# Where SBUF tiles begin: multiples of 256 bytes, and sixteen operand tiles in steps of 16

## The chip, the cores and the metric

The kernel runs on one NeuronCore of a Trainium2 chip. The metric is the device time in microseconds (us) of one execution. A time is the median of several runs.

## What is computed

A trunk of two decoder layers on 512 tokens of width 1024, batch 1, all in float32:

```python
for i in range(2):
    if i == 0:
        u = rms_norm(h, conv_norm_g)
        h = h + conformer_conv(u, ...)       # pw1 (1024 -> 2048), GLU, causal depthwise conv (31 taps),
    else:                                    # layer norm, SiLU, pw2 (1024 -> 1024)
        u = rms_norm(h, attn_norm_g)
        h = h + diff_attention(u, ...)       # 8 heads, QK norm, T5 bias, two softmaxes per head, w_o
    u = rms_norm(h, ffn_norm_g[i])
    h = h + (silu(u @ w_gate[i]) * (u @ w_up[i])) @ w_down[i]      # 1024 -> 2816 -> 1024
    gate = sigmoid(rms_norm(h, ple_norm_g[i]) @ ple_w_gate[i])
    h = h + gate * (p[i] @ ple_w_proj[i])
```

## The kernel before

**Layout.** Activations are kept transposed: `h[c]`, c = 0..7, holds 128 of the 1024 channels on the partitions and the 512 tokens along the row. A tile of 128x512 float32 takes 2048 bytes of a partition.

**Products in three.** Each float32 operand is split into a high part rounded to float32r and a low part, the remainder. `mm3` (lines 139 to 143) makes one product of them with three matmuls into the same PSUM tile: low x high (line 141), high x low (142), high x high (143). In TensorE's operation one operand is *stationary* (loaded as weights by LDWEIGHTS, 128 columns of it at a time, 512 bytes of a partition) and the other *moves* (512 columns, 2048 bytes of a partition). In nearly all of the kernel the weight matrix is stationary (tiles `whi`, `wlo`, 128x1024, of which column block k is used at step k of the sum) and the activation moves. In the projection to q, k and v (`tokens`) it is the other way round: the norm's tile is stationary, a half of `whi` or `wlo` moves.

**Norm tiles.** A norm (class `Norm`) writes for each chunk c the scaled activation in two tiles, high `A{2c}` and low `A{2c+1}`: sixteen tiles A0 to A15. `split_scaled` (lines 154 to 156) fills them from ScalarE and VectorE. The same sixteen tiles hold the convolution's output ahead of pw2 (`z`) and the heads' outputs ahead of w_o (`ot`, `stage_o`). The hidden activations of an FFN lie in B0 to B7, each with its high and its low half in one buffer of 4096 bytes.

**The stream.** Weights come by DMA on the Sync queue into `wraw` (two buffers), ScalarE rounds them to `whi`, VectorE or GpSimd subtracts to `wlo` (four buffers each). The framework's scheduler orders each engine's instructions; the stages are pw1 with the depthwise convolution between, pw2, the FFN (gate and up, then down, in three parts of 8, 8 and 6 blocks), the gated embedding, then QKV with attention's stages between, w_o, and FFN and embedding again. The last output tile of the kernel is done in two cuts of 256 columns.

**Where tiles begin.** A pool gives each tag its buffers in the order in which the tags first come up, each rounded up to 32 bytes. Ahead of all lie a scratch area of 2048 bytes for DMA descriptors and four constants of 32 each. Then come `vec` (416), `ident` (512), `ones` (512), four `wk` (2048 each) and `mhalf` (32). That makes 11840 = 46 x 256 + 64. The tiles that follow are all of 2048 or 4096 bytes: `h`, `acc`, `wraw`, `whi`, `wlo`, A0 to A15, `wth`, `wtl`, `bias`. So each of these begins 64 bytes past a multiple of 256. Then come the small `v8` and `r8`, two of 32 bytes each, so that `rb`, `big`, C0 to C3, B0 to B7 and D0 to D5 begin 192 bytes past one. C4, which came up earlier, begins at 64; C5, behind the 32 bytes of `lam`, at 224.

Of the kernel before, what the change touches and what calls it, by code (L numbers as in the profile page):

```python
# [13 lines left out]
F32R = mybir.dt.float32r  # L14
# [6 lines left out]
P = 128  # L21
S = 512
# [23 lines left out]
NV = _at  # L46
# [26 lines left out]
def trunk(ctx, tc, xT, pT, wts, diag, dww, vec, rel, onehot, lamv, out):  # L73
    nc = tc.nc
    V, A, G, T = nc.vector, nc.scalar, nc.gpsimd, nc.tensor
# [7 lines left out]
    def sb(shape, tag, bufs, dt=F32):  # L83
        uid[0] += 1
        return pool.tile(shape, dt, tag=tag, name=f"{tag}_{uid[0]}", bufs=bufs)
# [9 lines left out]
    big = lambda dt=F32, shape=(P, S): sb(list(shape), "big", 5, dt)  # L95
    f = lambda ap: ap.bitcast(F32)


    vt = sb([P, NV], "vec", 1)
    nc.scalar.dma_start(vt, vec)  # L100

    def col(name, i=0):
        a, _ = VEC[name]
        return vt[:, a + i : a + i + 1]
# [2 lines left out]
    make_identity(nc, ident)  # L107
    ones_r = sb([P, P], "ones", 1, F32R)
    ones = f(ones_r)
    t = wk()[:, 0:P]  # L110
    V.memset(t, 1.0)
    V.tensor_copy(ones_r, t)
    mhalf = sb([P, 8], "mhalf", 1)
    V.memset(mhalf, -0.5)


    t = tp()
# [36 lines left out]
    def split_scaled(src, scale, hi, lo):  # L154
        A.activation(hi, src, AF.Copy, scale=scale)
        V.scalar_tensor_tensor(lo, src, scale, f(hi), ALU.mult, ALU.subtract)  # L156

    class Norm:
# [4 lines left out]
            self.eng = acc_engine or G  # L163

        def chunk(self, c):
            hi = sb([P, S], f"A{2 * c}", 1, F32R)
            lo = sb([P, S], f"A{2 * c + 1}", 1, F32R)
            split_scaled(h[c], col(self.g, c), hi, lo)
            self.u.append((hi, lo))
            if c == 0:  # L170
                A.activation(self.acc, h[c], AF.Square)
            else:
                sq = wk()
                A.activation(sq, h[c], AF.Square)
                self.eng.tensor_tensor(self.acc, self.acc, sq, ALU.add)  # L175

        def columns(self):

            t = tp()
            for b in range(4):  # L180
                T.matmul(t[:, b : b + 1], self.acc[:, b * P : (b + 1) * P], ones[:, 0:1], start=True, stop=True)  # L181
            return rsqrt_cols(t[:, 0:4], 4, 1.0 / D)
# [11 lines left out]
    last_pow = [None]  # L194

    def rsqrt_cols(src, n, inv):
        v = sb([P, 8], "v8", 2)
        last_v[0] = V.tensor_scalar(v[:, :n], src, inv, EPS, ALU.mult, ALU.add)
        r = sb([P, 8], "r8", 2)
        last_pow[0] = G.tensor_tensor(r[:, :n], v[:, :n], mhalf[:, :n], ALU.pow)  # L200
        return r[:, :n]

# [173 lines left out]
        moments(NC - 2)  # L376
    moments(NC - 1)

    vs = sb([P, 8], "v8", 2)
    junk = wk()  # L380
    for at, t in ((4, sums["mean"]), (0, sums["sq"])):
        for b in range(4):
# [4 lines left out]
    V.tensor_tensor(vs[:, 4:8], vs[:, 4:8], vs[:, 4:8], ALU.mult)  # L387
    V.tensor_tensor(vs[:, 0:4], vs[:, 0:4], vs[:, 4:8], ALU.subtract)
    lrow = spread(diagonal(rsqrt_cols(vs[:, 0:4], 4, 1.0)))
    with tc.issue_after(last_v[0].ins), tc.issue_after(last_pow[0].ins):  # L390
        drow = wk()
# [22 lines left out]
    z = []  # L414
    with tc.manual_schedule(engines={V.engine, A.engine}):
        for c in range(NC + 2):
            if c < NC:
                V.tensor_tensor(y[c], y[c], lrow, ALU.mult)
                A.activation(y[c], y[c], AF.Silu, scale=col("ln_g", c), bias=col("ln_b", c))
                z.append((sb([P, S], f"A{2 * c}", 1, F32R), sb([P, S], f"A{2 * c + 1}", 1, F32R)))  # L420
                A.copy(z[c][0], y[c])
            if c >= 2:
                V.tensor_tensor(z[c - 2][1], y[c - 2], f(z[c - 2][0]), ALU.subtract)
# [139 lines left out]
    def tokens(ws, tb, between=()):  # L563
        acc = mm()
        for k in range(NC):
            a = tuple(t[:, tb * P : (tb + 1) * P] for t in u[k])
            mm3(acc, a, ws[k], k == 0, k == NC - 1)
            if k < len(between) and between[k]:
                between[k]()
        if rcol[0] is None:  # L570
            r = sb([P, 4], "rcol", 1)
            V.tensor_copy(r, norm.columns())
            rcol[0] = r
        return acc, rcol[0][:, tb : tb + 1]
# [15 lines left out]
    def unit(pair, ws, tb, between):  # L590

        if tb == 0:
            qk[pair] = [sb([P, 2, S], f"C{i}", 2, F32R) for i in range(6)]

            for c in range(2):
                G.memset(f(qk[pair][4 + c][HALVES[1 - c]]), 0.0)  # L596
        acc, r = tokens(ws, tb, between)
        q = big()
        A.activation(q, acc, AF.Copy, scale=r)
        sq = wk()  # L600
        if SQ_ACT:
            A.activation(sq, acc, AF.Square, scale=r)
        else:
            G.tensor_tensor(sq, q, q, ALU.mult)
        ss = sb([P, 8], "v8", 2)
        V.tensor_reduce(out=ss, in_=sq.rearrange("p (g d) -> p g d", g=8), op=ALU.add, axis=AX.X)
        rs = rsqrt_cols(ss, 8, 1.0 / DH)
        q3 = q.rearrange("p (g d) -> p g d", g=8)
        G.tensor_tensor(q3, q3, rs.unsqueeze(2).to_broadcast([P, 8, DH]), ALU.mult)
        return pair, tb, q  # L610
# [78 lines left out]
    def stage_a(hd, qb):  # L689
        if qb % 2 == 0:  # L690
            oacc[hd, qb // 2] = mm()
        o = oacc[hd, qb // 2][:, (qb % 2) * 2 * P : (qb % 2 + 1) * 2 * P]
        hi, lo = state[hd, qb]
        for k in range(qb + 1):
            cut = slice(k * P, (k + 1) * P)
            T.matmul(o, hi[:, cut], val[hd, k], start=(k == 0), stop=False)  # L696
            T.matmul(o[:, 0:P], lo[:, cut], val[hd, k][:, 0:P], start=False, stop=(k == qb))  # L697
        if qb % 2 == 1:
            if qb == 1:
                osb[hd] = sb([P, S], f"D{hd % 6}", 1)  # L700
            half = osb[hd][:, (qb // 2) * 2 * P : (qb // 2 + 1) * 2 * P].rearrange("p (a d) -> p a d", a=2)
            t4 = oacc[hd, qb // 2].rearrange("p (a c d) -> p a c d", a=2, c=2)
            A.copy(half, t4[:, :, 1])
            V.tensor_tensor(half, t4[:, :, 0], half, ALU.add)
        if qb == 3:
            o_ = osb[hd]
            sq = wk()
            A.activation(sq, o_, AF.Square)
            ss = sb([P, 8], "v8", 2)
            V.tensor_reduce(out=ss[:, 0:4], in_=sq.rearrange("p (g d) -> p g d", g=4), op=ALU.add, axis=AX.X)  # L710
            r0 = sb([P, 4], "r0", 1)
            V.reciprocal(r0, stats[hd][:, :, 2])
            V.tensor_tensor(ss[:, 0:4], ss[:, 0:4], r0, ALU.mult)
            V.tensor_tensor(ss[:, 0:4], ss[:, 0:4], r0, ALU.mult)
            rs = rsqrt_cols(ss[:, 0:4], 4, 1.0 / P)
            V.tensor_tensor(rs, rs, r0, ALU.mult)
            o3 = o_.rearrange("p (g d) -> p g d", g=4)
            G.tensor_tensor(o3, o3, rs.unsqueeze(2).to_broadcast([P, 4, P]), ALU.mult)
# [3 lines left out]
    def stage_o(hd):  # L722
        t = tp()
        for i in range(4):
            T.transpose(t[:, i * P : (i + 1) * P], osb[hd][:, i * P : (i + 1) * P], ident)  # L725
        hi = sb([P, S], f"A{2 * hd}", 1, F32R)
        lo = sb([P, S], f"A{2 * hd + 1}", 1, F32R)
        split_scaled(t, gains[:, 1:2], hi, lo)
        ot[hd] = (hi, lo)

# [3 lines left out]
    for n in range(len(todo) + LA):  # L734
        for stage, at in ((stage_s, n), (stage_t, n - LT), (stage_a, n - LA)):
            if 0 <= at < len(todo):
                stages.append((n, partial(stage, *todo[at])))
# [6 lines left out]
    for what, at, pace in QKV:  # L744
        ws = slab(GLO if at > 0 else 0)
        for tb in range(4):
            between = take(3 * pace[tb])
            between += [None] * (6 - len(between))
            if waiting:
                between.append(partial(unit_end, *waiting))  # L750
                waiting = None
            if what == "v":
                values(at, ws, tb, between)
            else:
                waiting = unit(at, ws, tb, between)
# [5 lines left out]
    def step():  # L761
        if stages:
            n, s = stages.pop(0)
            s()
        else:
            n = 99
        while done[0] < NH and (n - LA - 3) // 4 > done[0]:
            stage_o(done[0])
            done[0] += 1
# [150 lines left out]
```

## Time and profile before

| | |
|---|---|
| median of 3 runs | 1330.34 us (1330.23 to 1330.62) |
| profiled execution | 1331.2 us |
| its span, first to last instruction | 1329.4 us |
| mean granted TensorE clock | 0.983 |
| TensorE (PE) busy | 1291.5 us, 97% |
| weight loads (PEld), beside PE | 1038.7 us, 78% |
| VectorE (DVE) busy | 778.4 us, 59% |
| ScalarE (ACT) busy | 547.7 us, 41% |
| GpSimd (POOL) busy | 303.3 us, 23% |

In the profile's rows a matmul's tiles are written `mm<-A,whi`: the PSUM tile, then the tiles read, with their buffer numbers left out. L141 is line 141 of the kernel. `xN` is a count. In rows of groups, "| 425.4, 395" is the busy time of the group in us and the mean length of one in ns. In rows of the timeline the first number is the start in us, the second the length. Matmuls overlap: one starts before the previous has ended, so their pace is read from the distance of starts.

### The profile page before, as it was taken

Reading aid. Unit: us, or ns where it says so; the run is one execution under the profiler, and the core shown is the slowest. Engines: PE = TensorE matmul, PEld = TensorE weight load, DVE = VectorE, ACT = ScalarE, POOL = GpSimd, SP = SyncE. Lnnn points to the kernel's source line nnn. Section 1 sums busy time; section 2 is a strip of 40 time slices with the busy share of each in tenths; the row PEclk is TensorE's granted clock in tenths of the full one; section 3 lists DMA queues with packets and bytes.
Section 4 is the critical chain, followed back from the end, with each engine's and each line's share of the span. In section 5 each row is a group of like instructions: output and inputs, shape, how many; then the busy total and the mean of one; then the engine's idle time right before and its main releaser. Section 6 shows DMA issues by size and latency. Waiting matters only on the chain. (4 is left out here: it accounts for less than half of the span.)

```text
span 1329.4 us, 15025 instructions
## 1 busy us (share of the span) xinstructions
PE 1291.5 (97%) x5686; PEld 1038.7 (78%) x5686; DVE 778.4 (59%) x1203; ACT 547.7 (41%) x862; POOL 303.3 (23%) x241
## 2 busy tenths in 40 slices
PE   8999879999999999999999998999999999999998
PEld 6766458888888888888888886878888888888887
DVE  6999984644344434455678897946543344334445
ACT  5676453422123222244466766734322222223332
POOL 5789842100000000022254544122000000000030
PEclk7999889999999999999999999899999999999999
DMA  6231113233333332233222221213333233222231
GB/s 221 91 102 51 51 32 96 89 100 97 95 96 96 95 95 95 80 103 102 86 64 85 98 80 47 89 40 119 96 97 97 94 103 101 96 94 89 78 120 64
DMA packets 37332, 120.40 MB, mean 91 GB/s; under 512 B 4323, under 2 KB 5475, under 8 KB 37260
## 3 DMA queue, kind: packets, MB, share of 16 engines
q1 hardware_dynamic: 35712, 117.06, 27.5%
q10 hardware_dynamic: 1548, 2.39, 0.6%
q8 instruction: 44, 0.72, 0.2%
q14 instruction: 28, 0.23, 0.1%
HBM read 117.31 MB, written 2.12 MB: 90 GB/s over the span
## 5 line engine op out<-in xcount | busy, mean ns | idle before, releaser
L135 ACT CAST whi<-wraw 128x1024 fp32r<-128x1024 f32 (+2 forms) x214 | 218.4, 1025 | 568.2 <-PE mm L143 367.1
L141 PE MATMUL mm<-A,wlo 128*128 128x512 f32 (+1 forms) x1096 | 427.3, 394 | 10.4 <-POOL C L596 5.8
L142 PE MATMUL mm<-A,whi 128*128 128x512 f32 (+1 forms) x1096 | 430.0, 393 | 0.3 <-DVE A L156 0.3
L143 PE MATMUL mm<-A,whi 128*128 128x512 f32 (+1 forms) x1096 | 428.2, 391 | 0.0
L136 DVE TENSOR_TENSOR wlo<-wraw,whi 128x1024 fp32r<-128x1024 f32 (+2 forms) x207 | 258.9, 1254 | 63.2 <-ACT whi L135 63.0
L141 PEld LDWEIGHTS mm<-A,wlo 128*128 128x128 f32 x1096 | 207.8, 190 | 57.1 <-POOL C L596 6.6
L175 POOL TENSOR_TENSOR acc<-acc,wk 128x512 f32<-128x512 f32 x42 | 68.4, 1628 | 790.5 <-issue 676.8
L142 PEld LDWEIGHTS mm<-A,whi 128*128 128x128 f32 x1096 | 208.1, 190 | 46.3 <-issue 2.8
L143 PEld LDWEIGHTS mm<-A,whi 128*128 128x128 f32 x1096 | 207.8, 190 | 44.6 <-issue 1.9
L143 PE MATMUL mm<-B,whi 128*128 128x512 f32 x352 | 139.1, 395 | 0.0
L142 PE MATMUL mm<-B,whi 128*128 128x512 f32 x352 | 139.0, 395 | 0.0
L141 PE MATMUL mm<-B,wlo 128*128 128x512 f32 x352 | 138.4, 395 | 0.0
L304 POOL TENSOR_TENSOR wk<-wk,C 128x512 f32<-128x512 f32 x76 | 111.4, 1470 | 26.7 <-ACT C L303 20.6
L479 DVE TENSOR_TENSOR h<-mm,h 128x512 f32<-128x512 f32 x48 | 33.0, 692 | 128.0 <-PE mm L143 127.8
L471 DVE TENSOR_TENSOR big<-mm,rb 128x512 f32<-128x512 f32 x44 | 30.4, 691 | 125.9 <-PE mm L143 125.9
L469 DVE TENSOR_TENSOR big<-mm,rb 128x512 f32<-128x512 f32 x44 | 30.4, 691 | 99.4 <-PE mm L143 93.0
L143 PEld LDWEIGHTS mm<-B,whi 128*128 128x128 f32 x352 | 66.1, 188 | 16.1
L142 PEld LDWEIGHTS mm<-B,whi 128*128 128x128 f32 x352 | 66.1, 188 | 16.0
L141 PEld LDWEIGHTS mm<-B,wlo 128*128 128x128 f32 x352 | 66.1, 188 | 16.0
L143 PE MATMUL mm<-whi,A 128*128 128x512 f32 x192 | 75.6, 394 | 0.0
L142 PE MATMUL mm<-wlo,A 128*128 128x512 f32 x192 | 75.0, 396 | 0.0
L141 PE MATMUL mm<-whi,A 128*128 128x512 f32 x192 | 74.8, 396 | 0.0
(185 smaller groups left out, 1439.0 us busy)
## 6 DMA issues: line engine op xcount, KB each, us to landing
wraw<-in_wts SPq DMA_DIRECT2D x194, 512.0 KB, 3.5
wraw<-in_wts SPq DMA_DIRECT2D x16, 384.0 KB, 3.1
h<-in_xT SPq DMA_DIRECT2D x8, 256.0 KB, 5.8
bias<-scr ACTq DMA_DIRECT2D x8, 256.0 KB, 3.4
D<-in_diag SPq DMA_DIRECT2D x7, 256.0 KB, 4.0
out_t<-h SPq DMA_DIRECT2D x7, 256.0 KB, 2.0
wraw<-in_wts SPq DMA_DIRECT2D x4, 256.0 KB, 5.1
wraw<-in_pT SPq DMA_DIRECT2D x4, 256.0 KB, 2.6
```

What stands on the lines that cost most here:

```text
L135: A.copy(hi[:, cut], raw[:, cut])
L136: eng.tensor_tensor(lo[:, cut], raw[:, cut], f(hi[:, cut]), ALU.subtract)
L141: T.matmul(acc, al, bh, start=first, stop=False)
L142: T.matmul(acc, ah, bl, start=False, stop=False)
L143: return T.matmul(acc, ah, bh, start=False, stop=last)
L175: self.eng.tensor_tensor(self.acc, self.acc, sq, ALU.add)
L304: G.tensor_tensor(pacc, pacc, pr, ALU.add)
L469: V.tensor_tensor(tg, pg, rb, ALU.mult)
L471: V.tensor_tensor(tu, pu, rb, ALU.mult)
L479: V.tensor_tensor(h[m], acc, h[m], ALU.add)
```

## The change

Scratch and small tiles are padded so that every large tile begins at a multiple of 256 bytes: the scratch shrinks to 1024 bytes, `vec` gets 896, `mhalf` 1024 and is allocated (and set) ahead of `wk`, `v8` and `r8` get 256 for each buffer. Together, 1024 + 128 + 896 + 512 + 512 + 1024 = 4096, where `wk` begins. (The two buffers of tag C5, allocated behind `lam`, begin 32 bytes past a multiple.) The sixteen A tiles get 2304 bytes each, nine times 256, and tile i uses the 2048 that begin 16 x i bytes into them. So A0 begins at a multiple of 256, A1 16 bytes past one, and A15 240 past one.

```diff
-
-    vt = sb([P, NV], "vec", 1)
+    def atile(i):
+
+        return sb([P, S + 64], f"A{i}", 1, F32R)[:, 4 * i : 4 * i + S]
+
+    vt = sb([P, 224], "vec", 1)[:, :NV]
     nc.scalar.dma_start(vt, vec)
...
     ones_r = sb([P, P], "ones", 1, F32R)
     ones = f(ones_r)
+    mhalf = sb([P, 2 * P], "mhalf", 1)[:, :8]
+    V.memset(mhalf, -0.5)
     t = wk()[:, 0:P]
     V.memset(t, 1.0)
     V.tensor_copy(ones_r, t)
-    mhalf = sb([P, 8], "mhalf", 1)
-    V.memset(mhalf, -0.5)
...
         def chunk(self, c):
-            hi = sb([P, S], f"A{2 * c}", 1, F32R)
-            lo = sb([P, S], f"A{2 * c + 1}", 1, F32R)
+            hi = atile(2 * c)
+            lo = atile(2 * c + 1)
             split_scaled(h[c], col(self.g, c), hi, lo)
...
-        v = sb([P, 8], "v8", 2)
+        v = sb([P, P // 2], "v8", 2)[:, :8]
...
-        r = sb([P, 8], "r8", 2)
+        r = sb([P, P // 2], "r8", 2)[:, :8]
...
-                z.append((sb([P, S], f"A{2 * c}", 1, F32R), sb([P, S], f"A{2 * c + 1}", 1, F32R)))
+                z.append((atile(2 * c), atile(2 * c + 1)))
...
-        hi = sb([P, S], f"A{2 * hd}", 1, F32R)
-        lo = sb([P, S], f"A{2 * hd + 1}", 1, F32R)
+        hi = atile(2 * hd)
+        lo = atile(2 * hd + 1)
         split_scaled(t, gains[:, 1:2], hi, lo)
...
-    nc = bacc.Bacc("TRN2", target_bir_lowering=False, num_devices=1, dynamic_dma_scratch_size=2048)
+    nc = bacc.Bacc("TRN2", target_bir_lowering=False, num_devices=1, dynamic_dma_scratch_size=1024)
```

The three other places where a `v8` tile is made change like the first.

More of the change, by code (lines that the diff above doesn't have):

```diff
@@ L377, in trunk @@
     moments(NC - 1)
-    vs = sb([P, 8], "v8", 2)
+    vs = sb([P, P // 2], "v8", 2)[:, :8]
     junk = wk()
@@ L604, in unit @@
             G.tensor_tensor(sq, q, q, ALU.mult)
-        ss = sb([P, 8], "v8", 2)
+        ss = sb([P, P // 2], "v8", 2)[:, :8]
         V.tensor_reduce(out=ss, in_=sq.rearrange("p (g d) -> p g d", g=8), op=ALU.add, axis=AX.X)
@@ L708, in stage_a @@
             A.activation(sq, o_, AF.Square)
-            ss = sb([P, 8], "v8", 2)
+            ss = sb([P, P // 2], "v8", 2)[:, :8]
             V.tensor_reduce(out=ss[:, 0:4], in_=sq.rearrange("p (g d) -> p g d", g=4), op=ALU.add, axis=AX.X)
```

## The prediction

> **What bounds the kernel now.** I read the page first, then the groups by form, then the timeline of TensorE alone at five places.
>
> ```profile
> span 1329.4 us, 15025 instructions
> PE 1291.5 (97%) x5686; PEld 1038.7 (78%) x5686; DVE 778.4 (59%) x1203; ACT 547.7 (41%) x862; POOL 303.3 (23%) x241
> ```
>
> TensorE is busy for 97% of the span, and no other engine for more than 59%. So the time is set by how far apart matmuls start. The groups by form tell which matmuls count (name of output, then of moving and stationary tile):
>
> ```profile
> L142 PE MATMUL mm<-A,whi 128*128 128x512 f32 x1080 | 425.4, 395 | 0.3 <-DVE A L156 0.3
> L143 PE MATMUL mm<-A,whi 128*128 128x512 f32 x1080 | 423.6, 393 | 0.0
> L141 PE MATMUL mm<-A,wlo 128*128 128x512 f32 x1080 | 422.8, 396 | 10.4 <-POOL C L596 5.8 <-ACT A L155 2.7 <-DVE wlo L136 1.8
> L143 PE MATMUL mm<-B,whi 128*128 128x512 f32 x352 | 139.1, 395 | 0.0
> L142 PE MATMUL mm<-B,whi 128*128 128x512 f32 x352 | 139.0, 395 | 0.0
> L141 PE MATMUL mm<-B,wlo 128*128 128x512 f32 x352 | 138.4, 395 | 0.0
> L143 PE MATMUL mm<-whi,A 128*128 128x512 f32 x192 | 75.6, 394 | 0.0
> L142 PE MATMUL mm<-wlo,A 128*128 128x512 f32 x192 | 75.0, 396 | 0.0
> L141 PE MATMUL mm<-whi,A 128*128 128x512 f32 x192 | 74.8, 396 | 0.0
> ```
>
> That is 3 x 1080 = 3240 matmuls with a norm tile moving, 3 x 352 = 1056 with a B tile moving (the FFN's down projections), and 3 x 192 = 576 in QKV, where a norm tile is stationary and the weight moves. Before them TensorE idles 10.7 us in all. The 393 to 396 ns are a matmul's whole length; they overlap, so only the distance between starts counts. Here it is where B gives way to A (start in us, length in us):
>
> ```profile
> 1048.22 0.39 PE L141 MATMUL mm<-A,wlo 128*128 128x512 f32 x1
> 1048.45 0.40 PE L142 MATMUL mm<-A,whi 128*128 128x512 f32 x1
> 1048.68 0.39 PE L143 MATMUL mm<-A,whi 128*128 128x512 f32 x1
> 1048.91 0.39 PE L141 MATMUL mm<-A,wlo 128*128 128x512 f32 x1
> ...
> 1050.95 0.39 PE L141 MATMUL mm<-A,wlo 128*128 128x512 f32 x1
> ```
>
> From 1048.91 to 1050.95 there are nine starts: 2.04 / 9 = 226.7 ns each, and this is how A runs on undisturbed. But the first three, just after B, took 0.69 / 3 = 230 ns. And B itself, in the steady middle of a down projection:
>
> ```profile
> 596.21 0.40 PE L141 MATMUL mm<-B,wlo 128*128 128x512 f32 x1
> 596.45 0.39 PE L142 MATMUL mm<-B,whi 128*128 128x512 f32 x1
> 596.68 0.40 PE L143 MATMUL mm<-B,whi 128*128 128x512 f32 x1
> ...
> 599.01 0.40 PE L141 MATMUL mm<-B,wlo 128*128 128x512 f32 x1
> ```
>
> Twelve starts in 2.80 us: 233.3 ns, for the same form, the same weights and the same clock. A and B differ in where they start: by the sizes of the tiles allocated ahead of them, the norm tiles and the weights start 64 bytes past a multiple of 256, B starts 192 past one. So an address does cost time here, and either the moving tile's own start does it or its distance from the stationary tile's (0 for A, 128 bytes for B). What the distance between starts consists of is seen in the first microseconds:
>
> ```profile
> 10.20:13.60 3.40, 3.40 (x10) 2.63 (x9) 3.40 (x3) 3.40 (x8) 2.93 (x3) 0.50 1.07 383
> ```
>
> ```profile
> 10.13 0.63 PE L143 MATMUL mm<-A,whi 128*128 128x512 f32 x1
> ...
> 12.26 0.63 PE L143 MATMUL mm<-A,whi 128*128 128x512 f32 x1
> ...
> 14.77 0.39 PE L143 MATMUL mm<-A,whi 128*128 128x512 f32 x1
> ...
> 16.85 0.39 PE L142 MATMUL mm<-A,whi 128*128 128x512 f32 x1
> ...
> 18.21 0.39 PE L142 MATMUL mm<-A,whi 128*128 128x512 f32 x1
> ```
>
> The first fence is the row of a window: the granted clock, third number from its end, is 0.50 there. The second is the timeline. Five starts from 10.13 to 12.26 take 426 ns each; half of that, 213 ns, is what 512 columns need at full clock. So 226.7 holds 13.7 ns of something that is no work of the array, and that half speed hides. From 14.77, at full clock, nine starts take 2.08 us, 231.1 ns each; only from 16.85 on (six starts in 1.36 us) it is 226.7. The offsets were the same all along. A regular stream thus has to settle into 226.7 and takes some nine matmuls to get there. The last tile shows of what kind the extra time is:
>
> ```profile
> 1319.15 0.28 PE L143 MATMUL mm<-A,whi 128*128 128x256 f32 x1
> ...
> 1320.23 0.28 PE L143 MATMUL mm<-A,whi 128*128 128x256 f32 x1
> ```
>
> Nine starts of half the columns in 1.08 us: 120.0 ns, against 106.7 for the columns. Again 13.3 ns, so it goes with each matmul (and its one weight load), not with the columns: the reading of the next weights gets in the way of the moving operand's. That is my reading; the rows show only the amounts.
>
> **The change part by part.** The profiled execution took 1331.2 us, 1.8 beyond its span; the median of the runs is 1330.34, so I add what follows to 1330.3. Instructions, their order on each queue and the bytes moved stay; one memset changes place. No wait is added.
>
> (1) A moving, 3240 matmuls. Weights now start at a multiple of 256. The high half of chunk c starts 32c bytes past one, the low half 32c + 16. The distance between moving and stationary tile, constant before, now changes from one matmul to the next (0, 16, 0, 32, 48, 32 ...). A stream that took nine like matmuls to settle gets no two chunks alike. The best row for "not settled" is the 231.1 ns after 14.77; the three starts after B (230) and, below, QKV (232.5) lie around it. I take 231.1: +4.4 ns x 3240 = +14.3 us. Ends: 213, if a changing distance avoids the meeting altogether, -13.7 x 3240 = -44 us; 238, the longer of B's two alternating steps (0.24 then 0.23, together 0.47), +11.3 x 3240 = +37 us. I stay far from the lower end because no row at full clock, disturbed or not, keeps below 226.7 for more than a step.
>
> (2) B moving, 1056. B and the weights now both start at a multiple of 256: distance 0, as A had. I take 226.7: -6.6 x 1056 = -7.0 us. Ends: 0, if not the distance is what counts; and 213, -20.3 x 1056 = -21 us, if a start at a multiple of 256 is the cure in itself.
>
> (3) QKV, 576. The weight moves from offset 0, the norm tile is stationary at its own offset. These stretches are broken up by attention's matmuls:
>
> ```profile
> 704.07 0.39 PE L143 MATMUL mm<-whi,A 128*128 128x512 f32 x1
> 704.29 0.39 PE L141 MATMUL mm<-whi,A 128*128 128x512 f32 x1
> ...
> 705.65 0.39 PE L143 MATMUL mm<-whi,A 128*128 128x512 f32 x1
> ...
> 708.19 0.40 PE L141 MATMUL mm<-whi,A 128*128 128x512 f32 x1
> ...
> 709.12 0.39 PE L143 MATMUL mm<-whi,A 128*128 128x512 f32 x1
> ```
>
> Seven starts from 704.07 to 705.65 take 225.7 ns each, four from 708.19 to 709.12 take 232.5: settled about half of the time. Losing that half: +2.3 x 576 = +1.3 us; the ends, from their mean of 229.1, are -9.3 (213 for all) and +5.1 (238 for all).
>
> (4) The other engines read and write at shifted starts. The depthwise taps already read at every multiple of 4 bytes:
>
> ```profile
> L312 DVE SCALAR_TENSOR_TENSOR sc<-C,C,sc 128x512 f32<-128x512 f32 x94 | 67.4, 750 | 1.0
> L156 DVE SCALAR_TENSOR_TENSOR A<-tp,lam,A 128x512 fp32r<-128x512 f32 x8 | 5.9, 746 | 5.0 <-ACT A L155 4.9
> ```
>
> The same form costs 750 ns with 94 reads at shifting starts and 746 ns at a fixed one: 4 ns, and DVE is idle for 41% of the span. Zero; were the cover gone, 56 writes of A x 4 ns = 0.2 us.
>
> (5) The memset of mhalf moves ahead of two others on DVE:
>
> ```profile
> 0.83 0.17 DVE L111 MEMSET wk<- 128x128 f32 x1 [0.83 <-PEq L909]
> 0.94 0.07 DVE L114 MEMSET mhalf<- 128x8 f32 x1
> 1.03 0.23 DVE L112 CAST ones<-wk 128x128 fp32r<-128x128 f32 x1
> 1.48 3.49 PEld L119 LDWEIGHTS tp<-ones,ident 128*128 128x128 f32 x18 [1.48 <-POOL ident masks.py:199]
> ```
>
> It took 0.07 us between the same two already, the cast ends at 1.26, and TensorE waits for POOL's ident until 1.48. Zero, with 0.2 us to spare. The smaller scratch serves descriptors made by GpSimd, and no queue of that kind is in the page. Landing times of loads may shift by tenths of a microsecond; zero.
>
> Sum: +14.3 - 7.0 + 1.3 = +8.6, so 1330.3 + 8.6 = 1338.9 us. The sum turns where A's mean lies 1.8 ns over 226.7, at 228.5.
>
> The Trainium skill ("SBUF — State Buffer", Who interferes with whom) gives TensorE two independent read ports, one for the moving operand and one for the weights, and says "PE and ACT never wait on anyone"; "TensorE: Matmul & The Clock Gate" (Back-to-back issue gap) has N/2.4 + 2.5, 215.7 ns for 512 columns, without regard to addresses. By these, moving tiles changes nothing and the sum is 1330. The trace disagrees with the 215.7 (226.7 and 233.3 here).
>
> **The rivals.** *Spreading the starts avoids the meeting* (faster). If moving and stationary reads collide because they begin at the same place in a 256-byte period, sixteen different starts keep fifteen apart. At 220 ns, half of the surplus: A -6.7 x 3240 = -21.7, QKV -9.1 x 576 = -5.2, B -7.0, so 1296; at the floor of 213 for A and QKV it would be 1270. For: 13.7 ns are there to be had. Against: B is 128 bytes apart, as far as can be in 256, and is slower. It decides from A's mean below 228.5.
>
> *The stagger is harmless, B gains* (faster): what counts is that starts lie on 32 or 64 bytes or the like, A stays at 226.7, B gets there: 1330.3 - 7.0 = 1323. Against: B's start lies on 64 bytes now.
>
> *Nothing happens*: A and B differ by something other than addresses (B's tiles hold two halves in one buffer). 1330; the rule cited above comes out here. Against it: the moving halves are each 2048 contiguous bytes, like A's.
>
> *A falls to B's worse step and B gains nothing*: 238 everywhere where the distance isn't 0, +37 + 5 over 1330 is 1372. For: B's 237 to 238 in every second step. Against: it is only every second.
>
> **How the numbers follow.** The forecast, A between 229.5 and 233.5 and B between settled and as now, spans +9.1 - 7.0 + 1.3 to +22 + 1.3, that is 1334 to 1354; I give it 0.53. Spread starts avoid the meeting 0.16, harmless stagger 0.14, nothing 0.06, worse step 0.11. A measurement of this kernel tells some 0.2% (2.7 us) from no change. Faster: 0.16 + 0.14 = 0.30. Same: 0.06, and 0.03 from the forecast's lower edge, 0.09. Slower: 0.61. For 8 in 10, about a tenth is left out at each end: 1305 keeps the harmless stagger and a third of the faster rival, 1360 the whole forecast and the better end of the worst one.
>
> **What would show it.** Right: in the later A stretches (around 1049 to 1070) starts that differ from chunk to chunk and repeat from one output tile to the next, with a mean of 230 to 233; in the down projections an even 226 to 227 in place of 0.24, 0.23; the four QKV rows without settled runs; DVE and ACT means unchanged. Wrong: A's starts even at 226.7 or below, or B still alternating.

## The result and the profile after

| | before | changed |
|---|---|---|
| median of five runs | 1330.23 us | 1337.3 us |
| lowest to highest | 1330.13 to 1330.62 | 1334.03 to 1338.59 |
| profiled execution, its span | 1331.2, 1329.4 | 1336.22, 1334.4 |
| mean granted clock | 0.983 | 0.990 |

The changed kernel takes 1.0050 times as long, with an interval of 1.0035 to 1.0064: slower by 7.1 us, where the prediction had +8.6. The first lines of the page after, and then the groups by form of the stationary and moving tiles (line numbers are five higher than before):

```profile
span 1334.4 us, 15025 instructions
PE 1295.1 (97%) x5686; PEld 1032.7 (77%) x5686; DVE 776.8 (58%) x1203; ACT 547.8 (41%) x862; POOL 303.8 (23%) x241
```

```profile
L148 PE MATMUL mm<-A,whi 128*128 128x512 f32 x1080 | 428.1, 397 | 0.0
L147 PE MATMUL mm<-A,whi 128*128 128x512 f32 x1080 | 427.1, 396 | 1.5 <-DVE A L161 1.4
L146 PE MATMUL mm<-A,wlo 128*128 128x512 f32 x1080 | 424.6, 397 | 10.8 <-POOL C L601 6.0 <-ACT A L160 3.1 <-DVE wlo L141 1.7
L148 PE MATMUL mm<-B,whi 128*128 128x512 f32 x352 | 137.1, 389 | 0.0
...
L148 PE MATMUL mm<-whi,A 128*128 128x512 f32 x192 | 76.1, 397 | 0.0
L147 PE MATMUL mm<-wlo,A 128*128 128x512 f32 x192 | 75.6, 399 | 0.0
L146 PE MATMUL mm<-whi,A 128*128 128x512 f32 x192 | 75.1, 398 | 0.0
```

The counts are the same, and the idle time ahead of A's matmuls went from 10.7 to 12.3 us only. What moved are the mean lengths: B from 395 to 389 ns, A and QKV up by 1 to 4. The lengths show that there is a shift; the distance between starts, which sets the pace, has to be taken from the timeline. First a stretch with A moving, then the middle of a down projection with B moving:

```profile
1055.88 0.39 PE L146 MATMUL mm<-A,wlo 128*128 128x512 f32 x1
1056.11 0.40 PE L147 MATMUL mm<-A,whi 128*128 128x512 f32 x1
...
1061.43 0.39 PE L146 MATMUL mm<-A,wlo 128*128 128x512 f32 x1
```

```profile
598.08 0.39 PE L146 MATMUL mm<-B,wlo 128*128 128x512 f32 x1
598.30 0.39 PE L147 MATMUL mm<-B,whi 128*128 128x512 f32 x1
598.53 0.39 PE L148 MATMUL mm<-B,whi 128*128 128x512 f32 x1
...
601.48 0.39 PE L146 MATMUL mm<-B,wlo 128*128 128x512 f32 x1
```

One output tile with A is 24 starts, all eight chunks: 5.55 us, 231.3 ns each (before: 226.7). For B 15 starts take 3.40 us, 226.7 ns each (before: 233.3). So the two classes changed places, and there are three times as many with A.

For the rest of the text I took the mean distance over all starts of full 512-column matmuls of a class, leaving out distances above 260 ns (those hold a wait or half clock). In the profile before, that leaves 3160 for A, 1056 for B and 538 for QKV:

| mean distance, ns | A moving | B moving | QKV, A stationary |
|---|---|---|---|
| before | 226.97 | 233.29 | 228.94 |
| changed | 231.48 | 226.81 | 231.67 |

A +4.51 x 3160 = +14.3 us, B -6.48 x 1056 = -6.8, QKV +2.73 x 538 = +1.5: +9.0 in all. The two profiled spans differ by 5.0. Where the other 4.0 goes is seen by comparing the start of each matmul in the two traces. From the 601st to the 3201st (197 to 773 us in the profile before) the changed kernel falls behind by 4.1 us, and the distances give 4.1; from the 4001st to the 5601st (945 to 1310 us) by 1.4, and they give 1.4. So all that is missing is missing in the first 197 us (2.2 us) and between 773 and 945 us (1.7). At the start the changed kernel even gets ahead: its 91st matmul begins at 30.73 us where it began at 32.71 before. The windows of the first 30 us, changed kernel and then before (the granted clock is the third number from the end):

```profile
0.00:30.00 30.00, 22.51 (x87) 15.98 (x88) 18.93 (x21) 16.55 (x26) 17.45 (x22) 1.00 0.64 224
```

```profile
0.00:30.00 30.00, 24.03 (x82) 17.96 (x83) 19.40 (x22) 16.43 (x26) 17.44 (x22) 0.80 0.67 227
```

The half-clock stretch that the prediction used lay inside this window in the execution before and is missing here. The kernels below have 0.89 to 1.00 in the same window, in no order of their addresses, so it is not the addresses that bring the half clock. By the 301st matmul (87 us) the lead is lost again, but in both parts more of the time before was at half clock: the granted clock is 0.92 against 0.97 in the first 200 us, and 0.93 against 0.95 from 815 to 920 us. Two kernels below that have all tiles at distance 0 also stand 2.1 us apart at the 601st matmul, so executions alone can differ by that much. It fits that the five runs of the changed kernel lie 4.6 us apart. On the other hand, this change and two kernels below with a slower A all take 2 to 3.5 us less than their distances sum to, which would fit waits that hide a part of the slower matmuls. No run separates the two.

### The profile page after: what moved, and what is told of

Its sections match the earlier page's. It is cut to its first block, busy times and chain, and to the rows that moved or that the text cites. A ratio compares the mean times of both kernels' runs of the same rounds, so it can differ in the third digit from the quotient of the medians.

```text
span 1334.4 us, 15025 instructions
## 1 busy us (share of the span) xinstructions
PE 1295.1 (97%) x5686; PEld 1032.7 (77%) x5686; DVE 776.8 (58%) x1203; ACT 547.8 (41%) x862; POOL 303.8 (23%) x241
## 5 line engine op out<-in xcount | busy, mean ns | idle before, releaser
L148 PE MATMUL mm<-B,whi 128*128 128x512 f32 x352 | 137.1, 389 | 0.0
L147 PE MATMUL mm<-B,whi 128*128 128x512 f32 x352 | 137.0, 389 | 0.0
```

Of the source, the lines that this page charges most:

```text
L147: T.matmul(acc, ah, bl, start=False, stop=False)
L148: return T.matmul(acc, ah, bh, start=False, stop=last)
```

## The experiments

Three theories give the same times for both kernels. **Distance**: what counts is how far the moving tile's start is from the stationary tile's, modulo 256 bytes; 0 is best. **Variation**: what counts is that the distance stays constant from matmul to matmul, the reason that the prediction gave for A. **Start**: what counts is the moving tile's own start (a multiple of 256, or 64 past one, is good; 192 past one is bad). Unless said otherwise, the edits are to the changed kernel. An interval stands with the ratio to the kernel before.

**All A tiles at a multiple of 256.** The padding stays, the stagger goes:

```diff
-        return sb([P, S + 64], f"A{i}", 1, F32R)[:, 4 * i : 4 * i + S]
+        return sb([P, S + 64], f"A{i}", 1, F32R)[:, 0:S]
```

> The changed kernel with the sixteen A tiles all starting at offset 0 of their 2304 bytes, so that moving and stationary tiles all begin at multiples of 256. Distance theory (the pace is set by the distance between the starts of moving and stationary tile, and 0 is settled): A at 226.7 ns as before, B at 226.7 as in the changed kernel, QKV back to 229: 1330.2 - 6.8 = 1323.4 us. Variation theory (only a distance that changes from one matmul to the next costs): the same, 1323.4. Start theory (a moving tile that begins at a multiple of 256 is read faster or slower for that alone): B, which is at 226.7 there, says A will be too, so the same again. If A falls below 226 ns, all three miss something.

1323.54 us, ratio 0.9951 (0.9934 to 0.9968). A 226.96 ns, B 226.67, QKV 229.13. The 24 starts of an output tile:

```profile
1057.95 0.39 PE L146 MATMUL mm<-A,wlo 128*128 128x512 f32 x1
...
1063.39 0.39 PE L146 MATMUL mm<-A,wlo 128*128 128x512 f32 x1
```

5.44 us, 226.7 ns each. So the stagger alone costs 13.8 us between these two kernels (1337.3 - 1323.5), and the padding alone is a gain of 6.7 on the 1330.25 of the kernel before that was measured with it. The A tiles still lie 2304 bytes, nine times 256, from one to the next, so whole multiples of 256 between moving and stationary tile do not count.

**All A tiles 128 bytes past.** The distance is constant now but not 0, which tells variation from distance:

```diff
+        return sb([P, S + 64], f"A{i}", 1, F32R)[:, 32 : 32 + S]
```

> The changed kernel with all sixteen A tiles 128 bytes past a multiple of 256, constant, weights at 0. Distance theory: A runs as B ran before, at the same 128 bytes from its weights, in alternating steps of 229 and 237, mean 233.3: 1330.2 + 6.4 x 3160 - 6.8 + QKV 1.5 = 1345 us. Variation theory: a constant distance settles, A at 226.7, 1323 us. Start theory: A begins at a multiple of 128, as good as 64 was, 226 to 227 ns, 1323 us; only 192 would be bad.

1341.28 us, ratio 1.0087 (1.0072 to 1.0102). A 232.98 ns, B 226.77, QKV 232.47. The same 24 starts:

```profile
1058.04 0.39 PE L146 MATMUL mm<-A,wlo 128*128 128x512 f32 x1
1058.27 0.40 PE L147 MATMUL mm<-A,whi 128*128 128x512 f32 x1
...
1063.64 0.39 PE L146 MATMUL mm<-A,wlo 128*128 128x512 f32 x1
```

5.60 us, 233.3 ns each, just as B had before. Sixteen tiles at one and the same offset are slower than sixteen different ones: variation is not the cause. In QKV, where A is stationary and the weight moves from a multiple of 256, the same 128 bytes cost 3.3 ns a matmul (232.47 against 229.13; 232.45 in the second kernel of the next experiment). The total is 3.7 us below what the distance theory expected. A's mean accounts for 1.0 of that ((233.3 - 232.98) x 3160); the rest is not in these distances.

**Other constant distances.** Each stage gets an offset of its own, so one kernel measures several. `attn_g`, whose tiles are stationary, is kept at 0 in the first and third kernel and at 128 in the second:

```diff
+    OFF = {'conv_g': 16, 'z': 32, 'ffn_g0': 48, 'ple_g0': 64, ...}
+    def atile(i, who):
+        o = OFF[who] // 4
+        return sb([P, S + 64], f"A{i}", 1, F32R)[:, o : o + S]
```

> A constant offset for each stage's A tiles, so that one run samples several distances: pw1 16, pw2 32, first FFN 48, first embedding gate 64, QKV 0 (there the A tile is stationary), w_o 80, second FFN 96, second embedding gate 112 bytes; weights and B at 0. Variation theory: 226.7 ns in every stage, 1323 us. Distance theory: each stage its own steady pattern, none at 226.7 but QKV's settled stretches, between 228 and 237 on average: 1330 to 1350 us, the two FFNs (1056 matmuls each) weighing most. Start theory: 16, 48, 80 and 112 are worse than 32, 64 and 96.

> The same with pw1 144, pw2 160, first FFN 176, first embedding gate 192, QKV 128 (stationary), w_o 208, second FFN 224, second embedding gate 240 bytes. Variation theory: 226.7 ns throughout, 1323 us. Distance theory: each stage its own steady pattern above 226.7, 1330 to 1350 us; a distance d and its complement 256 - d need not agree. Start theory: 192 gives B's old 233, the others by whether they are multiples of 32 or 64.

> A constant distance for each stage again, below 16 bytes this time: first FFN 4, second FFN 8, first embedding gate 12, w_o 20, second embedding gate 252, pw2 248, pw1 244, QKV 0. If lines of 16 bytes are what collides, 4, 8 and 12 behave like 0 (226.7 ns) or, with one line more for each moving row, slightly above, and 20 and 244 to 252 like 16 and 240 (231.7 and 233.3). If every byte of distance counts, all lie between 229 and 234. Total between 1325 and 1342 us.

1337.77, 1340.04 and 1342.19 us in one run each. By distance (bytes: mean ns; the FFN stages have 1053 matmuls each, the others 166 to 341; 0 and 128 are the FFN stages of the two kernels above):

| bytes: ns | bytes: ns | bytes: ns | bytes: ns |
|---|---|---|---|
| 0: 226.7 | 4: 236.6 | 8: 233.4 | 12: 228.9 |
| 16: 231.6 | 20: 236.0 | 32: 233.3 | 48: 233.2 |
| 64: 229.0 | 80: 231.1 | 96: 233.4 | 112: 231.0 |
| 128: 233.0 | 144: 233.2 | 160: 234.2 | 176: 231.9 |
| 192: 233.3 | 208: 233.8 | 224: 233.3 | 240: 233.3 |
| 244: 239.6 | 248: 233.3 | 252: 226.8 | |

The timelines of two stages with 1053 matmuls, both from the third kernel; 4 bytes in the first FFN and 8 in the second:

```profile
450.24 0.40 PE L149 MATMUL mm<-A,wlo 128*128 128x512 f32 x1
...
455.21 0.40 PE L149 MATMUL mm<-A,wlo 128*128 128x512 f32 x1
```

```profile
1057.91 0.40 PE L149 MATMUL mm<-A,wlo 128*128 128x512 f32 x1
...
1063.51 0.40 PE L149 MATMUL mm<-A,wlo 128*128 128x512 f32 x1
```

21 starts in 4.97 us are 236.7 ns each, 24 in 5.60 are 233.3. The short stages hold longer starts of their own: with all tiles at distance 0 they have 226.9 to 228.0 where the FFN stages have 226.7, so a difference of 1 ns in the table means nothing. No distance beats 0; only 252, four bytes below it, equals it. A single element upwards costs 10 ns. So it is not that lines of 16 bytes collide: 4, 8 and 12 would then have behaved nearly like 0. The table also shows that variation adds nothing to the mean: over the sixteen distances of the changed kernel, counting the high tiles (even multiples of 16) twice, as `mm3` uses them, the constant distances average 232.2 ns. The changed kernel has 231.5.

**Everything at 192.** `vec` gets 192 bytes more on top of the kernel with A aligned, so the weights, A and B all start 192 past a multiple of 256, where B was slow before:

```diff
-    vt = sb([P, 224], "vec", 1)[:, :NV]
+    vt = sb([P, 224 + 48], "vec", 1)[:, :NV]
```

> The aligned kernel of the first experiment with vec 192 bytes longer, so that every tile behind it, weights, A and B, begins 192 bytes past a multiple of 256: the start at which B ran at 233.3 ns, but at distance 0. Distance theory: nothing changes against the aligned kernel, A and B at 226.7 ns, 1323.5 us. Start theory (192 is a bad place for a moving tile to begin, 64 or 0 a good one): A and B at 233.3, 1323.5 + 6.6 x 4296 = 1352 us.

1323.1 us, ratio 0.9941 (0.9927 to 0.9956); A 226.97, B 226.67, QKV 229.02.

```profile
1058.12 0.39 PE L146 MATMUL mm<-A,wlo 128*128 128x512 f32 x1
...
1063.56 0.39 PE L146 MATMUL mm<-A,wlo 128*128 128x512 f32 x1
```

Again 5.44 us for 24 starts. The start theory is dead: a moving tile 192 past is as fast as any if the weights are there too. (The weights' own start does not decide either: in the kernel before, the same start served A at 226.97 and B at 233.29.) Nor does a multiple of 256 help by itself, as the "large tiles begin at multiples of 256" of this change might suggest.

**The stagger without the padding.** The kernel before, with only the A tiles changed:

```diff
+    def atile(i):
+        return sb([P, S + 64], f"A{i}", 1, F32R)[:, 4 * i : 4 * i + S]
...
-            hi = sb([P, S], f"A{2 * c}", 1, F32R)
+            hi = atile(2 * c)
```

> The kernel before, with only the sixteen A tiles moved, each 16 x i bytes into 2304; weights stay at 64 and B at 192. Distance theory: A at 231.5 as in the changed kernel (the same sequence of distances), QKV at 231.7, B unchanged at 233.3: 1330.2 + 4.5 x 3160 + 1.5 = 1346 us, and the two parts of the change add up: +15.7 for the stagger, -6.8 for the rest. Start theory: A now begins at 64 + 16 i, sums that differ from those of the changed kernel, and a mean of its own.

1342.71 us, ratio 1.0088 (1.0071 to 1.0105): +11.4 us over the kernel before that was measured with it (1331.28), where 15.7 were expected. A 231.52 ns, B 232.41, QKV 231.73.

```profile
L146 PE MATMUL mm<-A,whi 128*128 128x512 f32 x1080 | 428.7, 397 | 0.0
L146 PE MATMUL mm<-B,whi 128*128 128x512 f32 x352 | 139.0, 395 | 0.0
```

A's length rose as in the changed kernel and B's stayed at 395 ns: the two parts are separate. B's mean is 0.9 ns below that of before all the same, in each of its six stretches, with 128 bytes between it and its weights as before. So the distance modulo 256 does not fix the pace to the last nanosecond (128 bytes have 232.4, 233.0 and 233.3 in three kernels); what else does is open. Here too less arrives in the time than the distances sum to (+4.55 x 3160, -0.88 x 1056 and +2.79 x 538 are +14.9), as for the whole change.

**The smallest edit that aligns B.** In the kernel before, only the tiles behind `r8` are out of step, by 128 bytes; two buffers of 96 bytes in place of 32 put them right:

```diff
-        r = sb([P, 8], "r8", 2)
+        r = sb([P, 24], "r8", 2)[:, :8]
```

> The kernel before with one number changed: each of the two r8 buffers gets 96 bytes in place of 32, so that everything allocated behind them (rb, big, C0 to C3, B, D) begins 64 bytes past a multiple of 256, like the norm tiles and the weights. Nothing is aligned to 256 and no A tile moves. Distance theory: A stays at 226.7 ns, B goes from 233.3 to 226.7: 1330.2 - 6.9 = 1323.4 us, the whole gain of the aligned kernel. If a start at a multiple of 256 were needed: 1330.

1322.71 us (1321.95 to 1324.62), ratio 0.9946 (0.9932 to 0.9959); A 226.98, B 226.67, QKV 229.15.

```profile
L143 PE MATMUL mm<-B,whi 128*128 128x512 f32 x352 | 136.9, 389 | 0.0
```

With weights, A and B at 64 past, it is 7.6 us faster than before and 14.6 faster than the changed kernel. This is the version to keep: the padding to 256 adds nothing to it.

**What the surplus over 213 ns is.** The prediction read it as the reading of the next weights. If so, half the weight columns should shrink it. With A aligned, the gates of both embeddings (but for the kernel's last output tile) use 64 of the 128 weight columns at steps 1 to 6, and leave out the other half of the result there:

```diff
+                    few = slice(0, DH) if cuts == 1 and 0 < k < NC - 1 else slice(0, P)
+                    mm3(acc[few], tuple(t[:, few] for t in wpart(w, k)), ...)
```

> The aligned kernel; in both embedding gates, but for the last output tile, steps 1 to 6 of 8 of the sum use only the first 64 columns of the weights (the outputs of the other 64 channels lack those steps). The moving operand and the array's 512 columns of work are unchanged, a weight load has 256 bytes of a partition in place of 512. If the 13.4 ns over 213.3 come from the weight load's reading, they halve: about 220 ns between such matmuls. If they belong to a matmul as such, 226.7 stays. In all 252 matmuls: 1321.9 or 1323.5 us.

```profile
1300.29 0.40 PE L146 MATMUL mm<-A,wlo 128*64 128x512 f32 x1
1300.52 0.39 PE L147 MATMUL mm<-A,whi 128*64 128x512 f32 x1
...
1304.43 0.39 PE L146 MATMUL mm<-A,wlo 128*128 128x512 f32 x1
```

1322.86 us in one run. 18 starts in 4.14 us are 230.0 ns each: neither the 220 of half the bytes nor an unchanged 226.7. The distances repeat 236, 229, 225, 226, 234, 230. The number of stationary columns does matter, which fits that the weights' reading takes part (the edit also halves the rows of the result that are written, and no run separates the two). But the surplus is not a price per byte of weights.

The last one asks for the pace of the loads alone, with the last output tile of the first embedding's gate in four cuts of 128 columns instead of one of 512. The edit reaches only this tile, 96 matmuls and not the 768 of its expectation, so its total says nothing about the totals that were expected; the distances do.

```diff
-    ple(n2, pp, lambda m, cut: norm.chunk(m))
+    ple(n2, pp, lambda m, cut: None if cut.stop < S else norm.chunk(m), 4)
```

> The aligned kernel with the first layer's embedding gate done in four cuts of 128 moving columns, so that 192 matmuls of 512 columns become 768 of 128 (the norm behind it takes its chunks after the last cut). The array's work is 53.3 ns each, a full weight load of 128 columns remains. If the surplus of 13.4 ns belongs to each matmul: 66.7 ns, 768 x 66.7 - 192 x 226.7 = +7.7 us, 1331 us. If it goes with the moving columns (6.3%): 56.7 ns, 1323.5. If the weight load's reading competes with the moving operand's for a full port, two equal streams would take twice the time: about 107 ns, 1362 us.

```profile
636.82 0.27 PE L146 MATMUL mm<-A,wlo 128*128 128x128 f32 x1
636.93 0.27 PE L147 MATMUL mm<-A,whi 128*128 128x128 f32 x1
...
639.50 0.28 PE L146 MATMUL mm<-A,wlo 128*128 128x128 f32 x1
```

1325.8 us in one run. 24 starts in 2.68 us are 111.7 ns each, where the columns need a quarter of 213, 53. Each matmul brings one load of 128 columns, and it is likely that this load now sets the pace. (The profile's rows for these loads are 192 ns long and overlap, so they do not give it.) The Trainium skill ("TensorE: Matmul & The Clock Gate", LDWEIGHTS) has P / 1.2 ns for P columns, an estimate of 106.7 for 128; the measured 111.7 is near it. The expectation's other reading, weights and moving columns read one after the other through one port, gives about 107 here too. But by the same account 512 columns would take an estimated (512 + 128) / 512 x 213 = 266 ns, and they take 226.7. At 111.7 ns a load, two fit into 226.7, so the load's duration is no bound with 512 columns, and yet where it reads from changes the pace.

## Why the prediction was right, and where its reason was not

- **The sum, +8.6, measured +7.1.** By its terms: A +14.3 forecast and +14.3 measured, B -7.0 and -6.8, QKV +1.3 and +1.5. The distances sum to +9.0; in the profiled pair 4.0 of this does not arrive, all of it in the first 197 us and between 773 and 945 us. The prediction let every nanosecond of a matmul count in full and everything else count nothing, so it did not have that.
- **Step (1), the amount.** 231.1 ns was taken from nine starts that followed the half-clock stretch; the measured mean is 231.5. The ends of 213 and 238 were not reached.
- **Step (1), the reason.** "A stream that took nine like matmuls to settle gets no two chunks alike" does not give the cost. That a stream at distance 0 has to settle after a disturbance stands, as QKV shows below. But a stream with all chunks alike, 128 bytes apart, runs at 233.3 ns without ever settling, and constant distances of 4 to 248 bytes have means of 229 to 240. It is the distance, not its change. So the step from "not settled" to 231.1 was wrong in its cause and right in its size. That the stagger's mean came out near the "not settled" row is luck in part: 226.7 is one value of a table in which nearly all others lie between 229 and 236.
- **Step (2)** said that B gains because its distance becomes 0, "as A had". The kernels with all tiles at 192 and with 128 bytes of padding show that this is the cause.
- **Step (3)** had QKV lose its settled half. It holds: before, 299 of the 538 distances are 226 or 227 ns, in runs of up to 35; in the changed kernel 71 are, never more than four in a row. The kernel with 128 bytes shows that the distance counts with the roles exchanged as well. The step's +2.3 ns comes from none of its rows (half of the 4.4 of step (1) would be 2.2, and from the mean of 229.1 to the unsettled 232.5 it is 3.4); 2.73 was measured.
- **Steps (4) and (5)** at zero. Of the forms that were quoted for step (4), in the profile after:

```profile
L317 DVE SCALAR_TENSOR_TENSOR sc<-C,C,sc 128x512 f32<-128x512 f32 x94 | 67.4, 751 | 1.0
L161 DVE SCALAR_TENSOR_TENSOR A<-tp,lam,A 128x512 fp32r<-128x512 f32 x8 | 5.9, 746 | 5.1 <-ACT A L160 5.0
```

  751 and 746 ns, where 750 and 746 were. For step (5), TensorE still begins at 1.49 us, when POOL's ident is there.
- **The reading of the surplus**, that the next weights' reading gets in the moving operand's way, is half borne out: the relation of both addresses counts, but half the weight columns made it 230.0 instead of less. What the two reads do to each other is open. A kernel that leaves weight loads out entirely was not tried.
- **The rivals.** Spreading the starts avoids no meeting: none of 23 distances is below 226.7. The harmless stagger would have given 1323, which is what the aligned kernel takes; A did not stay at 226.7. That A and B differ by something other than addresses is out, since 128 bytes of padding alone took B to 226.67. That nothing happens, which the prediction drew from the rule of the Trainium skill ("SBUF — State Buffer", Who interferes with whom) on TensorE's two independent read ports, is against 226.7 to 239.6 ns for one form at one clock. Whether the two reads meet at a port, no run shows. B did gain, so the worst case falls too.
- **What would show it.** The 24-start pattern repeats from tile to tile (5.55 us from 1055.88 and, in the next, from 1061.43 to 1066.98), its mean lies within 230 to 233, and B is even.

```profile
1066.98 0.39 PE L146 MATMUL mm<-A,wlo 128*128 128x512 f32 x1
```

## What to carry to other kernels

Where TensorE is the bound and each matmul brings its own weights, let the moving and the stationary tile begin at the same place modulo 256 bytes. Which place does not matter (0, 64 and 192 were tried, all with float32r operands), and a small buffer of odd size ahead of them is enough to lose it (in the kernel before, 96 bytes in place of 32 for each of two buffers were worth -0.54%). Look for it in the distance between matmul starts, by class of tiles, since busy shares (97% in all kernels here) do not show it and mean lengths only dimly. A change that does two things to addresses is to be costed as two terms: here -6.8 us were worth keeping and +15.8 were not.

## What was unexpected of the hardware

- The dependence is fine and not symmetric. Against the same stage at distance 0, 4 bytes up costs 9.9 ns a matmul (236.6 against 226.7), 4 bytes down (252) costs nothing (226.8 against 227.2), 12 bytes down (244) costs the most of all, 11.8 (239.6 against 227.8).
- In a sequence of changing distances single starts differ from what the same distance gives when constant: at an offset of 80, constant distance has a mean of 231.1 ns, while in the changed kernel the tile at 80 ran at 226. Only the means agree.
- The prediction took 213 ns for 512 columns from half clock. It can be had without that: with all at distance 0, 512 columns take 226.7 ns and 256 take 120.0 (the prediction's last tile), so 256 columns more cost 106.7, and 512 cost 213.4 if the surplus is the same for both. Twice that is 427, and at half clock starts were 426 apart: the surplus is not seen there at all.
- Fewer stationary columns made a matmul of 512 columns slower, 230.0 against 226.7 ns.
